# Sample attention on column tiles of 32 instead of 64: one chunk of features to a tile, four chunks side by side

## The chip, the cores and the metric

One Trainium2 chip, one core of it. The time is that of the device, in microseconds (us), for one execution of the whole step; of several runs the median is given.

## What is computed

A two-layer decoder trunk on a prompt of 1024 tokens and on 8 sample sequences of 8 tokens each, whose 2048 earlier keys and values lie in pages of 128 tokens in HBM. The change touches the attention of the samples in layer 0: 8 FoX heads of 64 features (a forget-gate bias is added to the scores) and 4 differential heads, each with two maps of 64 features (`q1.k1`, `q2.k2`) and values of 128 features. Cut to what matters:

```
s  = einsum('bqhd,bkhd->bhqk', qf, kf) * DH_FOX ** -0.5 + cq - ck      # FoX, 8 heads
s2 = einsum('bqhnd,bkhnd->bhnqk', qd, kd) * DH_DIFF ** -0.5            # differential, 4 heads x 2 maps
pf, pd = softmax(s), softmax(s2)          # over 2048 cached keys and the 8 new ones, masked
of = einsum('bhqk,bkhd->bqhd', pf, vf)
od = einsum('bhqk,bkhe->bqhe', pd[:, :, 0] - lam * pd[:, :, 1], vd)
```

For one sequence that is 8 tokens x 8 heads = 64 FoX rows and 8 tokens x 4 heads x 2 maps = 64 differential rows, 128 rows in all, against 2056 keys. All matrix products of the samples' attention are in fp32.

## The kernel before, in words

The work runs in stages: normalisation and projections (to about 285 us), then the last projections (of the values, `proj_v`) merged with the first 24 steps of the samples' attention, then the attention of the prompt merged with the rest of the samples', then output projection, recurrent block and feed-forward layers (from about 900 us).

**Layout.** The 512 FoX features and the 512 differential features of a token are each cut into four chunks `c` of 128; a chunk holds two FoX heads, or one differential head with its two maps. `hp` is the half of a chunk. Keys of a page lie as 128 features by 2 kinds by 4 chunks by 128 tokens (`kc`), values as 128 tokens by 2 kinds by 512 features (`vc`). The 128 rows of scores of a sequence are PSUM partitions: kind 0 (FoX) on partitions 0 to 63, kind 1 (differential) on 64 to 127.

**Scores.** `batch_start` (L825) writes a sequence's queries into `wz` (128 features x 2 kinds x 4 chunks x 64 columns), zero except where a chunk's features meet the rows of its own heads. `key_job` (L836) takes two pages: `load` (L839) reads them into one tile `raw` of 1 MB (two transfers of 512 KB from SyncE's queue; `RAW` = 5 such tiles rotate), and `mm` (L850) issues 8 products: for each chunk and kind, 64 columns of `wz` as the stationary operand, 256 key columns as the moving one, summed over the chunks into 64 partitions. A product with `csel` (L854) first adds the FoX bias from `cm`, which POOL loads (L844). `new_keys` (L867) does the same with the 8 new keys.

**Values.** `value_job` (L895) takes two pages of values: the probabilities are transposed (`turn`, L914), then for each page and kind a product with 64 columns of `pT` as stationary and all 512 features of the kind as moving operand (L932). Of the 64 x 512 that come out, each row needs the features of its own head alone. `end` (L935) scales, `end_sum` (L939) transposes four blocks of 128 and picks the needed parts into `mixs` and `ods`.

**Minus lambda.** `lamc` (L331 to L334) holds 1 for each row, and -lambda on the rows of the second map (partitions 96 to 127 before); `norm` (L889) multiplies it into the reciprocal sums.

**Order of the work.** `sample_jobs` (L951) lists key jobs of one sequence alternating with value jobs of the one before; `pipeline` (L615) runs a job's stages in successive steps (load, start, mm); `merge` (L968) interleaves the sample's steps with the prompt's by their share. SyncE's queue keeps this program order; on the other engines a scheduler sets the order of instructions with its own estimate of their durations. On POOL's queue stand, one behind the other, the loads of `cm`, the loads of the prompt's queries and keys (`load_map`, L590 and L591), and copies.

Of the kernel before, what the change touches and what calls it, by code (L numbers as in the profile page):

```python
# [11 lines left out]
F32 = mybir.dt.float32  # L12
F32R = mybir.dt.float32r
I32 = mybir.dt.int32
AF = mybir.ActivationFunctionType
OP = mybir.AluOpType
AX = mybir.AxisListType
# [5 lines left out]
TS = 64  # L23
T = TP + TS
NB = 8
NQ = 8
# [47 lines left out]
def sub_ap(t, off, dims):  # L74
    return bass.AP(tensor=t.tensor, offset=t.offset + off, ap=[list(t.ap[0])] + [list(d) for d in dims])
# [3 lines left out]
def hybrid_step(ctx: ExitStack, tc: tile.TileContext, xT, w_in, w_fl, w_v, w_out, w_gate, w_x, w_lout, w_ai, ffn_a, ffn_b,  # L79
# [3 lines left out]
    V, S, G, PE, SP = nc.vector, nc.scalar, nc.gpsimd, nc.tensor, nc.sync  # L83
# [38 lines left out]
    ident = const.tile([128, 128], F32, name="ident")  # L122
# [179 lines left out]
    qs = attp.tile([128, 2, 4, TS], F32, name="qs")  # L302
    kn = attp.tile([128, 2, 4, TS], F32, name="kn")
    cqT = attp.tile([128, 8, H], F32, name="cqT")
    lamc = attp.tile([128, 2], F32, name="lamc")
    csel = attp.tile([128, 128], F32R, name="csel")
# [3 lines left out]
    cqc = attp.tile([128, NB], F32, name="cqc")  # L310
# [5 lines left out]
    def attention_consts():  # L316
        SP.dma_start(ptt, ptab)
        SP.dma_start(newm, cst[:, CST["newm"][0]:CST["newm"][1]])
        lamp = tc.alloc_tile_pool(name="lamp", bufs=1, side="right")
        lraw = lamp.tile([128, 4, 64], F32, name="lraw")  # L320
        SP.dma_start(lraw, bass.AP(tensor=lamv.tensor, offset=lamv.offset, ap=[[0, 128], [64, 4], [1, 64]]))
        lsum = lamp.tile([128, 2], F32, name="lsum")
        lpr = lamp.tile([128, 2, 64], F32, name="lpr")
        V.tensor_tensor(lpr, lraw[:, 0:4:2], lraw[:, 1:4:2], op=OP.mult)
        V.tensor_reduce(lsum, lpr, axis=AX.X, op=OP.add)
        lex = lamp.tile([128, 2], F32, name="lex")
        S.activation(lex, lsum, AF.Exp)
        lam_init = 0.8 - 0.6 * math.exp(-0.3 * 0)
        lamt = lamp.tile([128, 1], F32, name="lamt")
        V.tensor_tensor(lamt, lex[:, 0:1], lex[:, 1:2], op=OP.subtract)  # L330
        V.tensor_scalar(lamc[:, 0:1], lamt, lam_init, -1.0, op0=OP.add, op1=OP.mult)  # L331
        lamp.release()
        V.memset(lamc[:, 1:2], 1.0)
        V.tensor_copy(lamc[96:128, 1:2], lamc[96:128, 0:1])  # L334
        V.tensor_scalar(gsub, vcol("subg"), 1.0 - lam_init, None, op0=OP.mult)

    qk_sc = [dram.tile([128, 2, TP], F32R, name=f"qk_sc{i}") for i in range(16)]
# [5 lines left out]
    cq_sc = dram.tile([H, TS], F32, name="cq_sc")  # L343
# [73 lines left out]
    csr = flp.tile([16, 128], F32, name="csr")  # L417
# [93 lines left out]
    for s, n in THIRDS:  # L511
        ps = bank("mm")
# [38 lines left out]
    G.dma_start(cn_sc[1], cl)  # L551
    SP.dma_start(cq_sc, fb[:, TP:])
    for h in range(H):
        SP.dma_start(cqc[h * NQ:h * NQ + NQ, :], bass.AP(tensor=cq_sc.tensor, offset=cq_sc.offset + h * TS, ap=[[1, NQ], [NQ, NB]]))
    S.copy(csel[0:16], csr)
    for i in range(2):
        G.dma_start(cmn[8 * i:8 * i + 8], cn_sc[i])

# [236 lines left out]
    sa1 = tc.alloc_tile_pool(name="sa1", bufs=1, side="right")  # L795
# [3 lines left out]
    mixs = sa1.tile([128, 4, TS], F32, name="mixs")  # L799
    ods = sa1.tile([128, 4, TS], F32, name="ods")  # L800
    bl = sa1.tile([128, KC, TS], F32, name="bl")
    wz = []
    for i in range(2):
        t = sa1.tile([128, 2, 4, 64], F32, name=f"wz{i}")
        G.memset(t, 0.0)
        wz.append(t)
    cms = []
# [17 lines left out]
    def batch_start(bt):  # L825
        b = bt["b"]
        w = bt["w"] = wz[b % 2]
        for kind in range(2):
            for hp in range(2):
                rows = slice(hp * 64, hp * 64 + 64)  # L830
                o, step = (hp * 8, 80) if kind == 0 else (hp * 32, 72)
                S.copy(sub_ap(w[rows], kind * 256 + o, [[step, 4], [1, NQ]]), qs[rows, kind, :, b * NQ:(b + 1) * NQ])
        bt["sx"] = sa.tile([128, PAST + NQ], F32, name="sx")
        bt["mx"] = small.tile([128, 5], F32, name="smx")

    def key_job(bt, g, u):  # L836
        jb = {}

        def load():  # L839
            jb["raw"] = load_keys(bt["b"], 4 * g + 2 * u)  # L840
            if u == 0:
                cm = bt["cm", g] = cms[flip["cm"] % 2]
                flip["cm"] += 1
                G.dma_start(cm[0:16], cs_sc[bt["b"], :, :, 4 * g:4 * g + 4, :].rearrange("i h j k -> (i h) (j k)"))  # L844

        def start():
            if g == 0 and u == 0:
                batch_start(bt)

        def mm():  # L850
            w = bt["w"]
            if u == 0:
                ps = bt["ps", g] = bank("ss")
                PE.matmul(ps, csel, bt["cm", g], start=True, stop=False, skip_group_check=True)  # L854
            ps = bt["ps", g][:, 256 * u:256 * u + 256]
            for c in range(4):
                for kind in range(2):
                    PE.matmul(ps[64 * kind:64 * kind + 64], w[:, kind, c, :], jb["raw"][:, :, kind, c, :], start=False,  # L858
                              stop=(c == 3), skip_group_check=True)

        def evac():
            V.tensor_tensor_reduce(out=bt["sx"][:, 512 * g:512 * g + 512], in0=bt["ps", g], in1=zero.to_broadcast([128, 512]),
                                   scale=1.0, scalar=-3e38, op0=OP.add, op1=OP.max, accum_out=bt["mx"][:, g:g + 1])
        return [load] + [None] * (LEAD - 1) + [start] + [None] * (GAP - 1) + [mm] + [evac] * u

    def softmax_job(bt):
        def new_keys():  # L867
            b, w, sx, mx = bt["b"], bt["w"], bt["sx"], bt["mx"]
            ps = bt["pn"] = bank("ss")
            bq = slice(b * NQ, (b + 1) * NQ)  # L870
            PE.matmul(ps[:, 0:NQ], csel, cmn[:, bq], start=True, stop=False, skip_group_check=True)
            for c in range(4):
                for kind in range(2):
                    PE.matmul(ps[64 * kind:64 * kind + 64, 0:NQ], w[:, kind, c, :], kn[:, kind, c, bq], start=False,
                              stop=(c == 3), skip_group_check=True)

        def top():
            ps, sx, mx = bt["pn"], bt["sx"], bt["mx"]
            V.tensor_tensor_reduce(out=sx[:, PAST:], in0=ps[:, 0:NQ], in1=newm, scale=1.0, scalar=-3e38,
                                   op0=OP.add, op1=OP.max, accum_out=mx[:, 4:5])  # L880
            nm = small.tile([128, 1], F32, name="snm")
            V.tensor_reduce(nm, mx, axis=AX.X, op=OP.max)
            cq = cqc[:, bt["b"]:bt["b"] + 1]
            V.tensor_tensor(nm, nm, cq, op=OP.add)
            V.tensor_tensor(nm, cq, nm, op=OP.subtract)
            bt["ls"] = small.tile([128, 1], F32, name="sls")
            S.activation(sx, sx, AF.Exp, bias=nm, accum_out=bt["ls"])

        def norm():  # L889
            rl = bt["rl"] = sa.tile([128, 1], F32, name="srl")  # L890
            V.reciprocal(rl, bt["ls"])
            V.tensor_tensor(rl, rl, lamc[:, 1:2], op=OP.mult)
        return [None] * (LEAD + GAP) + [new_keys, top, norm]

    def value_job(bt, g, x):  # L895
        jb = {}
# [26 lines left out]
        def mm():  # L923
            if x == 0 and late:
                turn()
            if g == 0 and x == 0:
                bt["po"] = bank("oo")
            pT, po = bt["pT", g], bt["po"]
            for jj in range(n2):
                for kind in range(2):  # L930
                    f = slice(64 * kind, 64 * kind + 64)
                    PE.matmul(po[f], pT[:rows, 2 * x + jj, f], jb["raw"][:rows, jj, kind],  # L932
                              start=(g == 0 and x == 0 and jj == 0), stop=(g == 4), skip_group_check=True)

        def end():  # L935
            bt["ob"] = sa.tile([128, 512], F32, name="ob", bufs=2)
            S.activation(bt["ob"], bt["po"], AF.Copy, scale=bt["rl"])

        def end_sum():  # L939
            b, ob = bt["b"], bt["ob"]  # L940
            bq = slice(b * NQ, (b + 1) * NQ)
            pt = bank("tt", (128, 4, 128))
            for c in range(4):
                PE.transpose(pt[:, c, :], ob[:, c * 128:(c + 1) * 128], ident)
            for hp in range(2):
                rows = slice(hp * 64, hp * 64 + 64)
                V.tensor_copy(mixs[rows, :, bq], sub_ap(pt[rows], hp * 8, [[144, 4], [1, NQ]]))
            V.tensor_reduce(ods[:, :, bq], sub_ap(pt, 64, [[136, 4], [1, NQ], [32, 2]]), axis=AX.X, op=OP.add)
        return [load] + [None] * (LEAD - 1) + [start] + [None] * (GAP - 1) + [mm] + ([end, end_sum] if g == 4 else [])

    def sample_jobs():  # L951
# [838 lines left out]
```

## Time and profile before

| | us |
|---|---|
| median of 3 runs (lowest to highest) | 3138.46 (3134.02 to 3145.78) |
| the profiled execution | 3136.24 |
| its span, first to last instruction | 3134.5 |
| TensorE busy | 2957.0 (94% of the span) |
| VectorE busy | 2100.7 (67%) |
| ScalarE busy | 1324.4 (42%) |
| GpSimd busy | 398.9 (13%) |

A row of a group of instructions reads: line, engine, operation, tile written <- tiles read, shape of operand, number of instructions. PE is TensorE's matmul, PEld its load of the stationary operand, SPq, POOLq and PEldq the instruction queue of the engine. An fp32 product of the program stands in the trace as two MATMUL records, each behind a load of its own, one for each pass of the fp32 product; one of kind fp32r (written `f32` in the rows too) is one record, and so is a transpose. "128\*64" is a stationary operand of 128 rows by 64 columns. A matmul's end is modelled, and consecutive ones overlap, so the time from start to start is what one costs.

### The profile page before, as it was taken

To read this page: it belongs to the slowest core of one execution; us is meant where nothing else is said; L and a number is where in the kernel's file an instruction comes from. 1 tells how busy PE (TensorE), PEld (TensorE's weight loads), DVE (VectorE), ACT (ScalarE), POOL (GpSimd) and SP (SyncE) were. 2 spreads that over 40 slices of the span, in tenths; PEclk is the share of its full clock that TensorE was granted. 3 is DMA by queue.
4 is the path that set the end of the run, shared out by engine and by line. 5 is a ranking of instruction groups with operands and counts; after the bars stand their busy time and mean duration, and the time that the engine had idled before them with its cause. 6 is when DMAs were issued, how large, how long until landed. Compare 5 with 4: busy or idle time off the path is not lost. (4 is left out here: it accounts for less than half of the span.)

```text
span 3134.5 us, 58133 instructions
## 1 busy us (share of the span) xinstructions
PE 2957.0 (94%) x21141; PEld 2709.5 (86%) x21141; DVE 2100.7 (67%) x4435; ACT 1324.4 (42%) x2477; POOL 398.9 (13%) x817
## 2 busy tenths in 40 slices
PE   7989999999997899899999999999969999999997
PEld 6988856565577899899999999999969899999997
DVE  6563134443458679988856777768785998886567
ACT  4111234444445533343344555555454334344444
POOL 0100010000000112321200011211011222221000
PEclk8999999999998999999999999999979999999999
DMA  4878688898785456544586652325735664448566
GB/s 147 238 226 308 208 324 306 308 338 319 274 263 191 161 174 207 199 143 140 175 269 193 216 184 96 100 97 167 262 126 172 221 209 161 151 145 260 181 187 212
DMA packets 383473, 646.96 MB, mean 206 GB/s; under 512 B 40305, under 2 KB 210690, under 8 KB 381138
## 3 DMA queue, kind: packets, MB, share of 16 engines
q1 hardware_dynamic: 321234, 478.65, 47.6%
q0 software_dynamic: 41792, 141.52, 12.2%
q10 hardware_dynamic: 20160, 23.07, 2.2%
q8 instruction: 166, 2.72, 0.4%
q14 instruction: 121, 0.99, 0.1%
HBM read 476.15 MB, written 166.95 MB: 205 GB/s over the span
## 5 line engine op out<-in xcount | busy, mean ns | idle before, releaser
L1060 ACT CAST b_hi<-b_raw 128x512 fp32r<-128x512 f32 (+1 forms) x645 | 394.8, 616 | 599.7 <-PE mm L1367 236.7
L136 DVE TENSOR_TENSOR b_lo<-b_raw,b_hi 128x512 fp32r<-128x512 f32 (+1 forms) x645 | 439.0, 683 | 236.6 <-ACT b_hi L1060 231.8
L1367 PE MATMUL mm<-d_lo,b_hi 128*128 128x272 f32 x1848 | 526.3, 293 | 4.6 <-DVE d_lo L136 4.5
L1368 PE MATMUL mm<-d_hi,b_lo 128*128 128x272 f32 x1848 | 525.2, 293 | 0.0
L1366 PE MATMUL mm<-d_hi,b_hi 128*128 128x272 f32 x1848 | 479.5, 297 | 40.7 <-ACT d_hi L1360 31.7
L1366 PEld LDWEIGHTS mm<-d_hi,b_hi 128*128 128x128 f32 x1848 | 331.4, 195 | 46.5 <-ACT d_hi L1360 40.6
L1367 PEld LDWEIGHTS mm<-d_lo,b_hi 128*128 128x128 f32 x1848 | 356.5, 193 | 6.4 <-DVE d_lo L136 6.2
L1368 PEld LDWEIGHTS mm<-d_hi,b_lo 128*128 128x128 f32 x1848 | 355.1, 193 | 0.0
L136 DVE TENSOR_TENSOR d_lo<-d_raw,d_hi 128x544 fp32r<-128x544 f32 (+1 forms) x297 | 175.5, 594 | 56.4 <-ACT d_hi L1360 55.2
L1360 ACT CAST d_hi<-d_raw 128x544 fp32r<-128x544 f32 (+1 forms) x297 | 160.8, 543 | 106.4 <-DMA d_raw<-a_b 50.0
L1082 PE MATMUL mm<-hh,b_hi 128*128 128x364 f32 (+1 forms) x480 | 158.5, 331 | 3.7 <-ACT b_hi L1060 3.1
L1083 PE MATMUL mm<-hl,b_hi 128*128 128x364 f32 (+1 forms) x480 | 157.6, 330 | 0.0
L1084 PE MATMUL mm<-hh,b_lo 128*128 128x364 f32 (+1 forms) x480 | 151.3, 330 | 0.0
L160 PE MATMUL mm<-hh,w_hi 128*128 128x364 f32 (+1 forms) x384 | 127.9, 335 | 14.4 <-DVE ev L296 7.9
L932 PE MATMUL oo<-raw,pT 128*64 128x512 f32 (+1 forms) x544 | 138.6, 604 | 1.1 <-ACT pT L921 1.1
L1211 PE MATMUL mm<-b22h,b_hi 128*128 128x272 f32 x384 | 115.0, 299 | 24.4 <-DVE bt L1294 24.4
L858 PE MATMUL ss<-raw,wz 128*64 128x256 f32 x1024 | 137.4, 389 | 0.0
L1271 ACT ACTIVATE ft<-ft 128x544 f32<-128x544 f32 x96 | 63.9, 666 | 169.1 <-DVE ft L1270 168.9
L161 PE MATMUL mm<-hl,w_hi 128*128 128x364 f32 (+1 forms) x384 | 127.9, 335 | 1.6 <-DVE hl L254 1.6
L162 PE MATMUL mm<-hh,w_lo 128*128 128x364 f32 (+1 forms) x384 | 127.3, 333 | 0.0
L675 ACT ACTIVATE st<-st,nb 128x128 f32<-128x128 f32 (+7 forms) x128 | 98.1, 768 | 55.2 <-DVE nb L669 29.4
L1212 PE MATMUL mm<-b22l,b_hi 128*128 128x272 f32 x384 | 114.1, 297 | 0.0
(401 smaller groups left out, 8401.6 us busy)
## 6 DMA issues: line engine op xcount, KB each, us to landing
raw<-in_kc SPq DMA_DIRECT2D x128, 512.0 KB
raw<-in_vc SPq DMA_DIRECT2D x128, 512.0 KB
b_raw<-w_sum SPq DMA_DIRECT2D x174, 256.0 KB
b_raw<-in_ffn_d SPq DMA_DIRECT2D x168, 256.0 KB
b_raw<-in_ffn_a SPq DMA_DIRECT2D x144, 256.0 KB
a_t<-ts POOLq DMA_DIRECT2D x116, 272.0 KB, 4.0
b_raw<-in_ffn_b SPq DMA_DIRECT2D x96, 256.0 KB
d_raw<-a_t SPq DMA_DIRECT2D x87, 272.0 KB
```

The lines of the kernel that those rows point to most:

```text
L136: (eng or V).tensor_tensor(out, x, hi, op=OP.subtract)
L160: PE.matmul(ps[:, :n], hi[:, k, :], rh[:, s:s + n], start=(k == order[0]), stop=False)
L858: PE.matmul(ps[64 * kind:64 * kind + 64], w[:, kind, c, :], jb["raw"][:, :, kind, c, :], start=False, stop=(c == 3), skip_group_check=True)
L932: PE.matmul(po[f], pT[:rows, 2 * x + jj, f], jb["raw"][:rows, jj, kind], start=(g == 0 and x == 0 and jj == 0), stop=(g == 4), skip_group_ ...
L1060: S.copy(hi, raw)
L1082: PE.matmul(ps[:, :n], hi, rh[:, s:s + n], start=(k == order[0]), stop=False)
L1083: PE.matmul(ps[:, :n], hi, rl[:, s:s + n], start=False, stop=False)
L1084: PE.matmul(ps[:, :n], lo, rh[:, s:s + n], start=False, stop=(k == order[-1]))
L1360: S.copy(rh, raw)
L1366: PE.matmul(p, wh[:, m, :], rh[:, s], start=(start and j == 0), stop=False, skip_group_check=True)
L1367: PE.matmul(p, wh[:, m, :], rl[:, s], start=False, stop=False, skip_group_check=True)
L1368: PE.matmul(p, wl[:, m, :], rh[:, s], start=False, stop=(j == nj - 1), skip_group_check=True)
```

## The change

The score rows are ordered by chunk: partition 32c + 8hp + q holds FoX head 2c + hp, and 32c + 16 + 8hp + q map `hp` of differential head c. Each chunk's products then write one band of 32 partitions, with `tile_position=(0, 32 * c)`.

- Scores: still 8 products of 256 columns for a key job, now with 32 stationary columns, kind outside and chunk inside, so that four products in a row go to four different column tiles. `wz` is half as wide.
- Values: for each page four products of 256 columns (the chunk's 128 FoX and 128 differential features) with 32 stationary columns, in place of two of 512 with 64.
- At a sequence's end 256 columns are scaled and two blocks transposed, not 512 and four.
- -lambda goes to partitions 32c + 24 to 32c + 31 by four small DMAs on POOL's queue, in place of one copy on VectorE; `cqc` and `csel` follow the new order of rows.

In the changed file lines 335 to 829 of before stand two lower, and those from 833 on one lower (L858 is L859 there, L932 is L933).

```
@@ attention_consts
-        V.tensor_copy(lamc[96:128, 1:2], lamc[96:128, 0:1])
+        for c in range(4):
+            r = slice(32 * c + 24, 32 * c + 32)
+            G.dma_start(lamc[r, 1:2], lamc[r, 0:1])
...
-        SP.dma_start(cqc[h * NQ:h * NQ + NQ, :], bass.AP(...))
-    S.copy(csel[0:16], csr)
+        SP.dma_start(cqc[32 * (h // 2) + 8 * (h % 2):32 * (h // 2) + 8 * (h % 2) + NQ, :], bass.AP(...))
+    S.copy(csel[0:16].rearrange("k (c a r) -> k c a r", c=4, a=2)[:, :, 0], csr[:, :64].rearrange("k (c r) -> k c r", c=4))
...
-        t = sa1.tile([128, 2, 4, 64], F32, name=f"wz{i}")
+        t = sa1.tile([128, 2, 4, 32], F32, name=f"wz{i}")
@@ batch_start
-                o, step = (hp * 8, 80) if kind == 0 else (hp * 32, 72)
-                S.copy(sub_ap(w[rows], kind * 256 + o, [[step, 4], [1, NQ]]), qs[rows, kind, :, b * NQ:(b + 1) * NQ])
+                S.copy(sub_ap(w[rows], kind * 144 + hp * 8, [[32, 4], [1, NQ]]), qs[rows, kind, :, b * NQ:(b + 1) * NQ])
@@ key_job, mm (new_keys likewise, with 0:NQ columns of kn)
-            for c in range(4):
-                for kind in range(2):
-                    PE.matmul(ps[64 * kind:64 * kind + 64], w[:, kind, c, :], jb["raw"][:, :, kind, c, :], start=False,
-                              stop=(c == 3), skip_group_check=True)
+            for kind in range(2):
+                for c in range(4):
+                    PE.matmul(ps[32 * c:32 * c + 32], w[:, kind, c, :], jb["raw"][:, :, kind, c, :], start=False,
+                              stop=(kind == 1), tile_position=(0, 32 * c), skip_group_check=True)
@@ value_job, mm
-                for kind in range(2):
-                    f = slice(64 * kind, 64 * kind + 64)
-                    PE.matmul(po[f], pT[:rows, 2 * x + jj, f], jb["raw"][:rows, jj, kind],
-                              start=(g == 0 and x == 0 and jj == 0), stop=(g == 4), skip_group_check=True)
+                for c in range(4):
+                    f = slice(32 * c, 32 * c + 32)
+                    PE.matmul(po[f, 0:256], pT[:rows, 2 * x + jj, f], jb["raw"][:rows, jj, :, 128 * c:128 * c + 128],
+                              start=(g == 0 and x == 0 and jj == 0), stop=(g == 4), tile_position=(0, 32 * c), skip_group_check=True)
@@ value_job, end and end_sum
-            S.activation(bt["ob"], bt["po"], AF.Copy, scale=bt["rl"])
+            S.activation(bt["ob"][:, :256], bt["po"][:, :256], AF.Copy, scale=bt["rl"])
...
-            for c in range(4):
-                PE.transpose(pt[:, c, :], ob[:, c * 128:(c + 1) * 128], ident)
+            for kind in range(2):
+                PE.transpose(pt[:, kind, :], ob[:, kind * 128:(kind + 1) * 128], ident)
```

How TensorE's order moves is shown at the place where the projections of values end and the prompt's first scores follow. Before (`raw,wz` are scores of cached keys, `raw,pT` values, `ident,sx` transposed probabilities, `qk` the prompt's scores):

```order
L854 MATMUL ss<-cm_2319,csel 128x512
L858 MATMUL ss<-raw,wz_2315 64x256 x16
L919 MATMUL tt<-ident,sx 128x128 x4
L919 MATMUL tt<-ident,sx 8x128
L932 MATMUL oo<-raw,pT 64x512 x9
L652 MATMUL ss<-qk 128x128
L654 MATMUL ss<-mask,identr 128x128
```

and with the change:

```order
L859 MATMUL ss<-raw,wz_2318 32x256 x16
L920 MATMUL tt<-ident,sx 128x128 x4
L920 MATMUL tt<-ident,sx 8x128
L933 MATMUL oo<-raw,pT 32x256 x16
L654 MATMUL ss<-qk 128x128
L656 MATMUL ss<-mask,identr 128x128
```

The products of a job stay together, as 32 columns by 256 in both kinds of job; the bias product L854 of this group moved to an earlier place.

On POOL's queue, at the same place, the prompt's first loads (`qk`, `kl`) stood behind nine loads of `cm`, before:

```order
L844 DMA cm_2319<-cs_sc 16x512
L844 DMA cm_2317<-cs_sc 16x512
L590 DMA qk<-qk_sc_92 128x2048
L591 DMA kl<-kl_sc_108 128x1024
L590 DMA qk<-qk_sc_93 128x2048
L591 DMA kl<-kl_sc_109 128x1024
```

and stand behind ten with the change:

```order
L845 DMA cm_2320<-cs_sc 16x512
L845 DMA cm_2322<-cs_sc 16x512
L592 DMA qk<-qk_sc_92 128x2048
L593 DMA kl<-kl_sc_108 128x1024
L592 DMA qk<-qk_sc_93 128x2048
L593 DMA kl<-kl_sc_109 128x1024
```

One more load of `cm`, which waits for the bias product two groups back, is now ahead of the prompt's first loads.

## Rows read from the trace of the kernel before

**Rows 1.** The page: span and busy time of TensorE and its weight loads, VectorE, ScalarE and GpSimd over the whole run; and of the DMA issues the one that loads pages of keys.

```profile
span 3134.5 us, 58133 instructions
PE 2957.0 (94%) x21141; PEld 2709.5 (86%) x21141; DVE 2100.7 (67%) x4435; ACT 1324.4 (42%) x2477; POOL 398.9 (13%) x817
...
raw<-in_kc SPq DMA_DIRECT2D x128, 512.0 KB
```

**Rows 2.** Stretches of the two merged stages: from and to, length, busy us of PE, PEld, DVE, ACT and POOL with the number of instructions, then the granted share of TensorE's clock, the DMA engines' busy share and GB/s.

```profile
285.00:350.00 65.00, 65.00 (x519) 51.07 (x519) 6.92 (x19) 13.21 (x24) 0.97 (x2) 1.00 0.81 305
350.00:400.00 50.00, 50.00 (x375) 40.40 (x376) 3.85 (x6) 8.38 (x15) 0.49 (x1) 1.00 0.55 177
400.00:450.00 50.00, 48.89 (x293) 26.74 (x291) 17.96 (x81) 17.52 (x44) 6.08 (x15) 0.93 0.94 343
450.00:500.00 50.00, 50.00 (x333) 29.55 (x332) 18.90 (x82) 24.25 (x56) 3.57 (x8) 1.00 0.80 277
500.00:550.00 50.00, 50.00 (x297) 30.73 (x295) 21.18 (x82) 20.23 (x46) 4.82 (x11) 1.00 0.92 347
550.00:600.00 50.00, 49.83 (x323) 29.19 (x322) 22.50 (x99) 24.97 (x58) 5.07 (x11) 1.00 0.94 347
600.00:650.00 50.00, 50.00 (x318) 30.16 (x316) 22.49 (x85) 23.19 (x51) 3.43 (x7) 1.00 0.90 323
650.00:700.00 50.00, 50.00 (x316) 31.59 (x315) 23.20 (x92) 19.35 (x44) 4.33 (x11) 1.00 0.84 300
700.00:750.00 50.00, 47.99 (x297) 27.59 (x294) 18.34 (x81) 22.92 (x55) 2.35 (x5) 0.97 0.79 276
750.00:800.00 50.00, 49.77 (x335) 33.07 (x335) 23.70 (x108) 22.43 (x49) 5.57 (x13) 1.00 0.93 344
800.00:850.00 50.00, 50.00 (x309) 27.49 (x305) 17.09 (x63) 19.65 (x46) 3.03 (x7) 1.00 0.86 318
850.00:900.00 50.00, 48.45 (x265) 27.38 (x265) 20.53 (x78) 24.66 (x50) 0.00 (x0) 1.00 0.64 212
```

**Rows 3.** The two stages again, for the instructions of one line alone (busy us of PE and PEld with the number of records; clock, DMA share and GB/s are the stretch's): first the products of cached keys, L858, then those of values, L932.

```profile
285.00:400.00 115.00, 28.54 (x224) 15.18 (x224) 1.00 0.69 249
400.00:900.00 500.00, 108.87 (x800) 57.38 (x800) 0.99 0.85 309
...
285.00:400.00 115.00, 11.40 (x48) 3.00 (x48) 1.00 0.69 249
400.00:900.00 500.00, 127.22 (x496) 33.08 (x496) 0.99 0.85 309
```

**Rows 4.** TensorE's matmuls in order of time, some 15 us of the second stage: start, length from the first start to the last end, what, how many records.

```profile
498.88 0.60 PE L944 MATMUL tt<-ident,ob 128*128 128x128 f32 x4
...
500.43 0.40 PE L652 MATMUL ss<-qk 128*128 128x512 f32 x1
500.67 0.39 PE L655 MATMUL ss<-kl,qk 128*128 128x512 f32 x1
...
502.12 3.65 PE L932 MATMUL oo<-raw,pT 128*64 128x512 f32 x16
505.71 1.13 PE L714 MATMUL tt<-pf,v 128*128 128x256 f32 x4
...
507.14 0.40 PE L854 MATMUL ss<-cm,csel 128*128 128x512 f32 x1
507.47 0.65 PE L858 MATMUL ss<-raw,wz 128*64 128x256 f32 x2
508.05 0.92 PE L714 MATMUL tt<-pf,v 128*128 128x256 f32 x4
508.90 3.67 PE L858 MATMUL ss<-raw,wz 128*64 128x256 f32 x30
```

**Rows 5.** The same view, one line: the products of one sequence's 8 new keys (8 moving columns).

```profile
314.77 0.64 PE L874 MATMUL ss<-kn,wz 128*64 128x8 f32 x16
```

**Rows 6.** From the list of waits on SyncE's queue from 285 to 900 us (who waited <- for what: us in total, times, longest): L818 issues the loads of pages. Then, from the view of the instructions that read or write `raw`, 400 to 900 us, what ended the idle time before them where it was a page's landing (us, times).

```profile
SPq L818 <- PE ss L858: 114.9, 35, 9.2
SPq L818 <- PE oo L932: 108.3, 41, 12.1
...
  DMA raw<-in_vc: 0.7, 3
```

**Rows 7.** Four successive stretches of 20 us, columns as in rows 2.

```profile
500.00:520.00 20.00, 20.00 (x113) 11.48 (x112) 10.04 (x37) 9.76 (x19) 2.66 (x5) 1.00 1.04 408
520.00:540.00 20.00, 20.00 (x117) 12.52 (x117) 6.78 (x26) 6.77 (x19) 1.32 (x4) 1.00 0.98 378
540.00:560.00 20.00, 20.00 (x142) 12.62 (x141) 9.86 (x56) 9.53 (x21) 1.63 (x5) 1.00 0.61 187
560.00:580.00 20.00, 19.83 (x130) 12.21 (x129) 11.39 (x38) 11.25 (x24) 3.31 (x7) 1.00 1.03 390
```

**Rows 8.** The instructions on `lamc`, with shortest, median and longest ns, and first and last start in us: the copy that the change removes, and the multiplication that reads the column (L892, in `norm`). Then POOL's first load of the prompt's queries and keys in order of time; in brackets, how long POOL's queue had been idle, and until what.

```profile
L334 DVE COPY lamc<-lamc x1: 149/149/149, 27.0 to 27.0; 32x1 f32<-32x1 f32 x1
L892 DVE TENSOR_TENSOR srl<-srl,lamc x8: 151/159/161, 320.3 to 858.5; 128x1 f32<-128x1 f32 x8
...
400.79 0.58 POOL L590 DMA_DIRECT2D qk<-qk_sc  x1 [34.98 <-PE ss L854]
```

More of the change, by code (lines that the diff above doesn't have):

```diff
@@ L553, in hybrid_step @@
     for h in range(H):
-        SP.dma_start(cqc[h * NQ:h * NQ + NQ, :], bass.AP(tensor=cq_sc.tensor, offset=cq_sc.offset + h * TS, ap=[[1, NQ], [NQ, NB]]))
-    S.copy(csel[0:16], csr)
+        SP.dma_start(cqc[32 * (h // 2) + 8 * (h % 2):32 * (h // 2) + 8 * (h % 2) + NQ, :], bass.AP(tensor=cq_sc.tensor, offset=cq_sc.offset + h * TS, ap=[[1, NQ], [NQ, NB]]))
+    S.copy(csel[0:16].rearrange("k (c a r) -> k c a r", c=4, a=2)[:, :, 0], csr[:, :64].rearrange("k (c r) -> k c r", c=4))
     for i in range(2):
@@ L871, in new_keys @@
             PE.matmul(ps[:, 0:NQ], csel, cmn[:, bq], start=True, stop=False, skip_group_check=True)
-            for c in range(4):
-                for kind in range(2):
-                    PE.matmul(ps[64 * kind:64 * kind + 64, 0:NQ], w[:, kind, c, :], kn[:, kind, c, bq], start=False,
-                              stop=(c == 3), skip_group_check=True)
+            for kind in range(2):
+                for c in range(4):
+                    PE.matmul(ps[32 * c:32 * c + 32, 0:NQ], w[:, kind, c, :], kn[:, kind, c, bq], start=False,
+                              stop=(kind == 1), tile_position=(0, 32 * c), skip_group_check=True)
         def top():
@@ L929, in mm @@
             for jj in range(n2):
-                for kind in range(2):
-                    f = slice(64 * kind, 64 * kind + 64)
-                    PE.matmul(po[f], pT[:rows, 2 * x + jj, f], jb["raw"][:rows, jj, kind],
-                              start=(g == 0 and x == 0 and jj == 0), stop=(g == 4), skip_group_check=True)
+                for c in range(4):
+                    f = slice(32 * c, 32 * c + 32)
+                    PE.matmul(po[f, 0:256], pT[:rows, 2 * x + jj, f], jb["raw"][:rows, jj, :, 128 * c:128 * c + 128],
+                              start=(g == 0 and x == 0 and jj == 0), stop=(g == 4), tile_position=(0, 32 * c), skip_group_check=True)
         def end():
             bt["ob"] = sa.tile([128, 512], F32, name="ob", bufs=2)
-            S.activation(bt["ob"], bt["po"], AF.Copy, scale=bt["rl"])
+            S.activation(bt["ob"][:, :256], bt["po"][:, :256], AF.Copy, scale=bt["rl"])
         def end_sum():
@@ L942, in end_sum @@
             pt = bank("tt", (128, 4, 128))
-            for c in range(4):
-                PE.transpose(pt[:, c, :], ob[:, c * 128:(c + 1) * 128], ident)
+            for kind in range(2):
+                PE.transpose(pt[:, kind, :], ob[:, kind * 128:(kind + 1) * 128], ident)
             for hp in range(2):
                 rows = slice(hp * 64, hp * 64 + 64)
-                V.tensor_copy(mixs[rows, :, bq], sub_ap(pt[rows], hp * 8, [[144, 4], [1, NQ]]))
-            V.tensor_reduce(ods[:, :, bq], sub_ap(pt, 64, [[136, 4], [1, NQ], [32, 2]]), axis=AX.X, op=OP.add)
+                V.tensor_copy(mixs[rows, :, bq], sub_ap(pt[rows], hp * 8, [[32, 4], [1, NQ]]))
+            V.tensor_reduce(ods[:, :, bq], sub_ap(pt, 144, [[32, 4], [1, NQ], [8, 2]]), axis=AX.X, op=OP.add)
         return [load] + [None] * (LEAD - 1) + [start] + [None] * (GAP - 1) + [mm] + ([end, end_sum] if g == 4 else [])
```

## The prediction

> **What bounds the kernel now.** I read the page first: TensorE is busy for 2957.0 of 3134.5 us, every other engine much less [rows 1]. That is an average, so next the table by stretches of the two stages in which the samples' attention runs, 285 to 900 us [rows 2]. Here PE is busy from edge to edge in nearly every stretch, while VectorE and ScalarE are at most half busy. The column to watch is another one: the DMA engines, at 0.79 to 0.94 from 400 to 850 us. The waits say how the two stand to each other: SyncE's loads of pages waited 114.9 us for the score products and 108.3 us for the value products, that is for a free `raw` tile, while PE's idle time that a page's landing ended is under a microsecond [rows 6]. So TensorE sets the pace now, and the transfers follow at 85% of what they can do after 400 us [rows 3]. A faster TensorE asks them for more.
>
> **What the narrow products cost now.** The two lines that change hold 1024 score records and 544 value records, by the counts of [rows 3]. In order of time [rows 4] 16 value records take 3.65 us, the last alone 0.6, so 3.05 / 7 = 0.43 us for two, start to start; 30 score records take 3.67 us, the last 0.38 of it, 3.29 / 14 = 0.235 for two. A value product moves 512 columns and a score product 256; half of 0.43 is 0.22, and I take that for the scores. For a full-width fp32 product of 256 columns the same view has four records in 1.13 us, the last 0.38 of it: some 0.22 us for one. So with 64 columns two records run at once, one on each half of the array. Are they two passes of one product, or the products of two kinds? One row decides: a score product that stands alone is two records in 0.65 us, which is 0.27 plus the 0.38 that one lasts, so its passes ran one after the other (at 507.47 us) [rows 4]. What runs side by side are two column tiles, and for that the second tile's first pass must start while the first tile's second pass, ahead of it in the program, is still waiting.
>
> **Removed from TensorE.** Scores: 512 pairs x 0.22 us = 113 us. Values: 272 pairs x 0.43 us = 117 us. Together 230 of the 276 us that the two lines are busy [rows 3]; the rest is filling and draining at each block's ends, and stays. With the change the score jobs have as many records of as many columns, the value jobs twice as many of half the columns. If four tiles run at once, four records share 0.22 us: 256 + 272 such groups, 528 x 0.22 = 116 us. That saves 114 us: by the counts of rows 3, 112 pairs x 0.11 + 24 x 0.215 = 17 us before 400 us, and 400 x 0.11 + 248 x 0.215 = 97 us after. Is the issue of so many short instructions a limit? The products of new keys, with 8 columns, show 16 matmuls and their 16 weight loads in 0.64 us, the last 0.2 of it [rows 5]: about 14 ns an instruction. A group of four is 8 instructions, 0.11 us, below the 0.22 us that its columns take. The new keys themselves have as many instructions as before: no gain.
>
> **Smaller edits.** A sequence's end saves two transposes of 0.11 us (at 498.88 us) [rows 4], eight times: 2 us, taken as it is; the shorter copy, the narrower `wz` and the other partitions of `cqc` and `csel` cost nothing, on engines half idle [rows 2]. The four DMAs for -lambda are issued at 27 us on POOL and needed first at 320 us [rows 8]; the column could be 290 us late before anyone waited. What they replace on VectorE is 149 ns.
>
> **Added to TensorE.** Widths change more often. By the order of instructions the stream goes from one width (128, 64, 32) to another 368 times before and 422 times after, because the prompt's products of 64 columns now stand beside blocks of 32. The lone block shows the price of a change: its first load stands 0.33 us behind the start of the 512-column product before it, where the next such product follows after 0.24 (at 507.14 and 500.43 us) [rows 4]; and the load after it comes 0.58 us after its start, where its two passes need 0.44. So 0.1 us for a change, 54 x 0.1 = 5 us; 3 where TensorE is still the bound.
>
> **What the transfers leave of it.** The pages' bytes are the same, so a stretch can get no shorter than its DMA busy time. The idle DMA time of the ten stretches after 400 us, length x (1 - share) [rows 2], is 3, 10, 4, 3, 5, 8, 10.5, 3.5, 7 and 18 us. TensorE would save 97 us there, 9.7 a stretch. The smaller of the two, stretch by stretch, is 3 + 9.7 + 4 + 3 + 5 + 8 + 9.7 + 3.5 + 7 + 9.7 = 62.6 us. That lets transfers shift freely within 50 us. They can't quite: five tiles of 1 MB are held, and at 400 GB/s [rows 7] a tile takes 2.6 us, so the stock is 13 us. At 20 us the shares are 1.04, 0.98, 0.61 and 1.03 [rows 7]; the smaller of 3.9 and the idle time is 0, 0.4, 3.9 and 0, 4.3 us in 80, which over 500 us would be 27. I take 50, nearer to 62.6, as a faster TensorE frees tiles earlier in the loose stretches and asks for the next there. Before 400 us the shares of 0.81 and 0.55 [rows 2] leave 35 us, more than the 17 that TensorE saves, which count in full.
>
> Where TensorE waits for pages its clock can fall. In the stretch from 400 us, the one with the lowest granted clock, 0.93 [rows 2], a seventh of 50 us was at the lower level, 1.2 in place of 2.4 GHz; that costs 3.5 us. One or two more such falls: 5 us.
>
> **The sum.** 17 + 50 + 2 - 3 - 5 = 61 us. The profiled execution took 3136.2 us, its span 3134.5 and 1.7 around it; 2.2 us under the median of 3138.5. 3136.2 - 61 = 3075; at the median's level 3077. I say **3076 us**. The ends of this case: with 27 in place of 50, and 12 in place of 17, it saves 33 us (3103); if the transfers were evened out over the whole of the second stage, up to its idle 72 us, some 95 us (3041).
>
> One rule of the Trainium skill would size the terms otherwise: TensorE: Matmul & The Clock Gate, Part 3, Measured speedup, gives 2.38x for three column tiles. An estimate from it: four tiles would win 4 x 0.79 = 3.2 over one, TensorE would save 86 us and the kernel some 50. The rows show for two tiles nearly the full factor.
>
> **The rivals.**
> *Two at a time still.* If the array, or what feeds it, takes only two streams, a job costs what it costs now, plus the 5 us of width changes: 3136.2 + 5 = 3141, no change. For it: no row has more than two at work. Against it: the dispatch past a waiting pass exists for two tiles [rows 4], and four need the same thing thrice. Its decision point: the length of a full block of 16 score records, 2.0 us if two run at once, 1.1 if four.
> The skill's rule in TensorE: Matmul & The Clock Gate, Part 3, What overlaps and what doesn't, is that matmuls are strictly first in, first out; then each tile's second pass would hold back the next tile, one product would need one 0.22 us step, and this rival would come true. The trace disagrees: 16 value records took eight steps (3.65 us), not the nine of such an order (4.1).
> *The transfers give nothing.* If the rate stays where it is after 400 us, because loads are issued in the program's order and each waits for its tile, the wait moves from SyncE to TensorE and only the first stage's 17 us remain, less 3 and 5: some 9 to 17 us, 3119 to 3127. For it: four stretches of rows 2 stand at 0.92 to 0.94. Against it: 408 GB/s is reached [rows 7] where 309 is the mean [rows 3].
> *One at a time: slower.* If narrow products with a named tile position don't overlap at all, each record costs its own 0.22 us: 1024 + 1088 records, 465 us in place of 230, with the width changes 240 us more on an engine that bounds the stage: 3136 + 240 = 3376. It decides from fewer than two tiles at work on average. For it: the overlap seen so far is of a form without such a position. Against it: those tiles too are bands of output partitions, only wider.
> *The prompt starts late.* Its first loads are now behind one more `cm` load on POOL. They went out at 400.79 us, when the projections ended [rows 8]; the bias products for which the added load waits stand ahead of the last projections in TensorE's order, so I put nothing.
>
> **How the numbers follow.** Forecast case 0.72; two at a time 0.14; transfers give nothing 0.08; one at a time 0.06. Half a per cent (16 us) is about what a measurement of this kernel can tell from no change. Faster: nearly all of the first (0.71) and half of the third (0.04), 0.75. The same: 0.14 + 0.04, 0.18. Slower: the fourth, and a little of the first, 0.07. The range runs from the forecast's lower end to the point of no change, 3041 to 3140: it leaves out the fourth case and the upper half of the second.
>
> **What would show it.** Right: 16 records of 32 columns in about 1.1 us, the two lines' busy time from 276 to some 160 us, the end of the second stage 60 us earlier, DMA shares of 0.95 in most of its stretches, SyncE's waits for the two lines well below 223 us, and PE's idle time by page landings in tens of us. Wrong: blocks of 16 score records still at 2.0 us; or the blocks short, but the stage as long as before, with TensorE waiting for something other than pages, VectorE or ScalarE above all.

## The result, and the profile after

The changed kernel takes 3061.9 us (median of 4 runs, 3060.3 to 3067.4) against 3140.7 for the kernel before beside it: ratio 0.9753, 95% interval 0.973 to 0.9777, faster by 79 us. Forecast were 3076 us and a range of 3041 to 3140. The profiled execution took 3062.7 us, 73.6 less than the one of before.

First the page: span and busy times, to set beside [rows 1].

```profile
span 3060.9 us, 59156 instructions
PE 2855.8 (93%) x21669; PEld 2659.7 (87%) x21669; DVE 2102.1 (69%) x4434; ACT 1326.3 (43%) x2477; POOL 402.8 (13%) x821
```

TensorE is busy 101 us less, with 528 matmul records more (544 more of values, 16 fewer transposes). Next its matmuls in order of time, where [rows 4] and [rows 5] stand for before (L859 are scores of cached keys, L875 those of new keys, L933 values).

```profile
446.24 1.07 PE L859 MATMUL ss<-raw,wz 128*32 128x256 f32 x16
449.32 1.07 PE L859 MATMUL ss<-raw,wz 128*32 128x256 f32 x16
...
453.36 0.31 PE L875 MATMUL ss<-kn,wz 128*32 128x8 f32 x16
...
454.19 0.64 PE L933 MATMUL oo<-raw,pT 128*32 128x256 f32 x8
```

A block of 16 score records, the two passes of eight products, takes 1.07 us: 0.38 for the last and 0.69 for three steps, 0.23 each. Two at a time would take 2.0 us. Eight value records take 0.64, one step and the last. Four column tiles run at once.

The table of the two lines, as in [rows 3]; the projections of values end at 380 us now (400 before) and the last value product at 816 (893).

```profile
285.00:380.00 95.00, 14.53 (x208) 5.54 (x208) 1.00 0.79 289
380.00:816.00 436.00, 54.34 (x800) 21.83 (x800) 0.96 0.96 356
...
285.00:380.00 95.00, 7.04 (x96) 2.62 (x96) 1.00 0.79 289
380.00:816.00 436.00, 77.91 (x992) 23.45 (x992) 0.96 0.96 356
```

Their busy time fell from 276 us to 154 (one block of scores, 1 us, now lies before 285 us). The clock and the DMA share are the other half of the story. Here is the whole second stage, from the end of the projections to the last value product, columns as in [rows 2]: before in the first row, after in the second, then four stretches after.

```profile
400.00:893.50 493.50, 489.98 (x3037) 289.81 (x3036) 205.52 (x842) 215.57 (x493) 38.25 (x87) 0.99 0.87 313
...
380.00:816.00 436.00, 409.42 (x3558) 251.11 (x3557) 206.28 (x851) 218.55 (x499) 37.67 (x86) 0.96 0.96 356
...
500.00:550.00 50.00, 48.82 (x448) 28.76 (x445) 22.26 (x89) 27.54 (x61) 4.92 (x12) 1.00 1.01 374
550.00:600.00 50.00, 44.38 (x386) 27.71 (x379) 29.10 (x116) 25.00 (x62) 5.01 (x11) 0.93 1.01 369
600.00:650.00 50.00, 50.00 (x458) 31.67 (x457) 21.21 (x86) 23.95 (x52) 4.64 (x11) 1.00 1.02 391
650.00:700.00 50.00, 44.76 (x352) 28.41 (x351) 26.79 (x101) 25.02 (x57) 4.13 (x8) 0.93 0.91 337
```

Over the stage the DMA engines' share went from 0.87 to 0.96, and the granted clock from 0.99 to 0.96. Three of the four stretches have no DMA time left, and two of the four show TensorE idle for over 5 us with the clock down. The clock's records have five falls to its lower level in this stage, 34 us in all; before, they have two, 10 us in all. Narrow windows show them, first the five, then the two of before:

```profile
390.00:400.00 10.00, 7.40 (x55) 4.54 (x54) 4.23 (x26) 5.22 (x16) 0.80 (x2) 0.50 1.05 395
492.00:496.00 4.00, 3.93 (x26) 2.65 (x26) 2.60 (x17) 0.48 (x1) 0.00 (x0) 0.57 1.03 372
588.00:595.00 7.00, 5.61 (x23) 4.99 (x22) 3.42 (x18) 3.41 (x13) 1.08 (x3) 0.51 1.04 394
690.00:697.00 7.00, 6.10 (x31) 3.78 (x32) 2.00 (x4) 1.17 (x2) 0.00 (x0) 0.53 1.05 392
786.00:793.00 7.00, 5.73 (x36) 3.59 (x37) 3.06 (x6) 4.69 (x10) 0.00 (x0) 0.51 1.00 397
...
414.00:421.00 7.00, 7.00 (x21) 4.03 (x22) 4.18 (x22) 5.26 (x12) 1.05 (x3) 0.51 1.04 394
714.00:718.00 4.00, 3.43 (x15) 2.81 (x17) 0.50 (x2) 2.75 (x6) 0.32 (x1) 0.57 0.81 270
```

The waits say what TensorE and the loads wait for (who waited <- for what: us, times, longest). First SyncE's queue in the second stage before (400 to 893.5 us), then after (380 to 816 us); in the fence behind it, TensorE's own idle time before matmuls in the second stage after.

```profile
SPq L818 <- PE ss L858: 94.3, 30, 7.6
SPq L818 <- PE oo L932: 93.8, 37, 12.1
SPq L818 <- DMA raw<-in_kc: 0.4, 1, 0.4
...
SPq L820 <- PE ss L859: 48.4, 26, 4.3
SPq L820 <- PE oo L933: 43.1, 30, 7.7
SPq L820 <- DMA raw<-in_vc: 19.5, 15, 3.3
SPq L820 <- DMA raw<-in_kc: 17.4, 6, 6.7
```

```profile
PE ss L654 <- DMA qk<-qk_sc: 5.7, 3, 2.6
PE tt L732 <- DVE st L700: 5.2, 5, 3.3
PE ss L657 <- DMA kl<-kl_sc: 3.4, 2, 2.0
PE ss L654 <- DVE mx L658: 3.2, 6, 1.0
```

The loads of pages wait 92 us for TensorE instead of 188, and now also for earlier pages to land (37 us against 0.4). TensorE does not wait much for pages: its idle time that they ended stays near 5 us over both stages. It waits for the prompt's queries and keys, 9 us, and for VectorE and ScalarE, the prompt's chain above all, some 15 us.

### The profile page after: what moved, and what is told of

The parts are those of the page before. It is cut to its first block, busy times and chain, and to the rows that moved or that the text cites. A ratio compares the mean times of both kernels' runs of the same rounds, so it can differ in the third digit from the quotient of the medians.

```text
span 3060.9 us, 59156 instructions
## 1 busy us (share of the span) xinstructions
PE 2855.8 (93%) x21669; PEld 2659.7 (87%) x21669; DVE 2102.1 (69%) x4434; ACT 1326.3 (43%) x2477; POOL 402.8 (13%) x821
## 5 line engine op out<-in xcount | busy, mean ns | idle before, releaser
L1367 PE MATMUL mm<-d_hi,b_hi 128*128 128x272 f32 x1848 | 486.1, 297 | 46.4 <-ACT d_hi L1361 34.2
L1214 PE MATMUL mm<-b22h,b_lo 128*128 128x272 f32 x384 | 115.8, 302 | 0.0
L1212 PE MATMUL mm<-b11h,b_hi 128*128 128x272 f32 x384 | 111.8, 291 | 0.0
```

The lines of the kernel that those rows point to most:

```text
L1212: PE.matmul(p[:, :NT], hi[:, k, :], rh, start=(start and k == 0), stop=False, skip_group_check=True)
L1367: PE.matmul(p, wh[:, m, :], rh[:, s], start=(start and j == 0), stop=False, skip_group_check=True)
```

## The experiments

All ratios are to the kernel before, run beside each kernel; the changed kernel's is 0.9753, and 0.9757 in a second measurement.

### Each half of the change alone

`keys_only` keeps the old value products, `values_only` the old score products (those of the new keys too, and the wider `wz`).

```
keys_only, value_job mm:      for kind: PE.matmul(po[64*kind ...], pT[..., f], raw[:rows, jj, kind], ...)      # 64 x 512, as before
values_only, key_job mm:      for c: for kind: PE.matmul(ps[64*kind ...], w[:, kind, c, :], ...)               # 64 x 256, as before
```

> The change for the scores alone: score products on four column tiles of 32, value products as before (two per page, 64 columns of probabilities by 512 features); the values' outputs then mix rows, only the time counts. Theory (TensorE saved some 120 us, the transfers kept a third of it): half the saving meets less of the transfers' limit, so it gets more than half of the full change's 77 us: about 45 us, 3093 us. Rival (each part gets its share of what chains between the engines allow): half, 39 us, 3100 us or above. Both: 16 score records in about 1.1 us, L859 busy about 69 us, value products still about 139 us.

> The change for the values alone: value products on four column tiles of 32, score products in the old form (64 columns, chunk outside, kind inside); the rows of scores then stand in the old order, only the time counts. Theory: about 43 us saved, 3096 us, so that the two halves alone add up to more (88 us) than the whole change (77). Rival: 38 us or less, and the sum at or below 77.

Measured: 3101.2 us, ratio 0.9895 (0.9877 to 0.9912), and 3097.1 us, 0.9875 (0.9857 to 0.9892). That is 33 and 39 us, together 72, within the error of the whole change's 77. The theory had expected more than half from each half, and this was a miss: the two parts add up. The second stage took 472 and 456 us (493 before, 436 with both). The traced execution of `values_only` took 3106.3 us, 9 over its median. The changed lines, as in [rows 3], first the scores of `keys_only`, then the values of `values_only`:

```profile
380.00:852.00 472.00, 57.15 (x800) 21.93 (x800) 0.97 0.90 327
...
393.00:849.00 456.00, 74.89 (x988) 24.26 (x992) 0.98 0.92 338
```

So already half the change lost much of its gain there: the scores alone cut their own line from 109 to 57 us in that stage and the stage by 21, with the DMA engines idle for a tenth of it. The prediction's smaller of two numbers per stretch (TensorE's saving, idle DMA time) is too simple: the loss sets in well before the stage's idle DMA time is used up.

### Are the transfers the limit? Fewer of them, and more

`half_after` and `half_before` leave out every second load of value pages, in the changed kernel and in the one before; `quarter_after` the same of keys as well; `extra_after` and `extra_before` load 33.5 MB twice.

```
half_*:     def load():  if x == 1: jb["raw"] = bt["vraw"]; return          # the tile of the job before
quarter_after, also:  if u == 0: bt["kraw"] = load_keys(...)
                      jb["raw"] = bt["kraw"]
extra_*:    if g < 4 and x == 0: load_pages(bt["b"], 4 * g, vc, more..., ...)  # a tile of its own, not read
```

> The changed kernel with every second load of value pages left out (the second value job of a group uses the tile of the first; 32 of 256 MB... that is 64 loads of 512 KB, 33.5 MB, are not made, and these values are wrong). Theory (transfers limit the second stage now): 30 to 45 us less than the changed kernel, 3062 to about 3025 us, DMA share in the second stage at 0.8 to 0.9, SyncE's waits for the products up again. Rival (TensorE's own order and its partners limit it): within 8 us of the changed kernel.

> The kernel before with the same loads left out. Theory: TensorE set the pace there, so the transfers cost little: 0 to 10 us less than before, 3130 to 3141 us. Rival (transfers were a limit before as well): over 20 us less.

> The changed kernel with every second load of pages left out for keys and values (67 MB in all; these scores and values are wrong). With half of that left out the second stage took 413 us and TensorE was busy for 400 of it. If that is TensorE's own floor, the stage stays at 400 to 413 us and the whole within 0 to 12 us of that kernel, 3030 to 3042 us. If transfers still held it, another 15 us or more go.

> The changed kernel with 33.5 MB more of transfers: each value job with x = 0 also loads its two pages into a tile of its own that nothing reads (64 loads of 512 KB, some 84 us of DMA at 400 GB/s). If the transfers are what the second stage now lacks (DMA busy 0.96 of its 436 us): 45 to 75 us slower than the changed kernel, 3105 to 3135 us. If TensorE's order and its partners hold it: under 20 us slower.

> The kernel before with the same loads added. Its two stages had some 100 us of idle DMA time, 65 of it in the second: 5 to 35 us slower than before, clearly less than the changed kernel loses. If the two lose the same, the transfers bind both alike.

| | us | ratio (95%) | second stage, us |
|---|---|---|---|
| half_before | 3136.7 | 1.0009 (0.9997 to 1.0021) | 499 |
| half_after | 3041.6 | 0.9691 (0.9666 to 0.9717) | 413 |
| quarter_after | 3043.6 | 0.9707 (0.9676 to 0.9738) | 421 |
| extra_before | 3172.2 | 1.0127 (1.0091 to 1.0162) | 532 |
| extra_after | 3123.5 | 0.9968 (0.9953 to 0.9984) | 506 |

The second stage of each, columns as in [rows 2]: `half_before`, `half_after`, `quarter_after`, `extra_before`, `extra_after`, one fence each.

```profile
397.00:896.00 499.00, 496.23 (x3034) 294.56 (x3034) 205.92 (x842) 215.99 (x493) 37.96 (x87) 0.99 0.72 250
```

```profile
377.00:790.00 413.00, 400.08 (x3508) 252.09 (x3506) 201.93 (x842) 211.95 (x492) 37.60 (x86) 0.98 0.85 302
```

```profile
379.00:800.00 421.00, 408.01 (x3519) 256.97 (x3517) 204.35 (x842) 213.07 (x493) 37.97 (x87) 0.96 0.67 232
```

```profile
394.00:926.00 532.00, 507.88 (x3101) 294.33 (x3099) 214.87 (x867) 224.23 (x505) 38.33 (x87) 0.97 0.95 352
```

```profile
379.00:885.00 506.00, 438.19 (x3588) 266.04 (x3586) 213.00 (x867) 223.41 (x505) 37.82 (x86) 0.91 0.98 368
```

Before, leaving out transfers gives nothing (TensorE busy 496 of 499 us, in an execution 16 us over the median): TensorE set the pace, as forecast. After, it gives 19 us (0.0062 of 3140), less than the 30 to 45 expected and more than the rival's 8. Leaving out twice as much gives no more: `quarter_after` lies a little above both of its ranges, with the DMA engines at 0.67 and TensorE busy for 408 of 421 us. So with fewer transfers the stage takes 413 to 421 us, 15 to 23 less than in the real kernel.

That size need not be the transfers' alone. Leaving out loads also made the scheduler place TensorE's instructions anew: set line by line beside the changed kernel's, the sequence of TensorE's records in these two traces differs in 2900 and 3100 lines. Three kernels with all loads and an order changed as much, at the end of this section, have stages 9 to 15 us longer than the changed kernel's.

Adding transfers costs the changed kernel 67 us of the 84 that the loads take, with the DMA engines at 0.98, well beyond the 16 to 27 us by which those three kernels are slower. The stage grew by 70 us: TensorE's idle time by 41, its busy time by 29. About as much was lost to the clock, 28 us (0.09 of 506 us instead of 0.04 of 436). The kernel before loses 40, a little over its range, though it had some 65 us of idle DMA time in the stage. So the transfers do bind now, and they bound little before.

### How far TensorE looks past a waiting product

`same_tile` puts four records in a row on the same column tile.

```
-            for kind in range(2):
-                for c in range(4):
+            for c in range(4):
+                for kind in range(2):
                     PE.matmul(ps[32 * c:32 * c + 32], w[:, kind, c, :], ..., tile_position=(0, 32 * c), ...)
```

> The changed kernel with the score products in the order chunk outside, kind inside, so that four records in a row go to one column tile; the values stay as changed. How far does TensorE look past a waiting record? If far (per-tile order with a deep queue): a block of 16 records still takes about 1.1 us and the time stays within 5 us. If one waiting record per tile can be passed: some 10 steps of 0.22 us, 2.4 us a block, 64 x 1.3 = 85 us more TensorE work, 40 to 80 us slower than the changed kernel. If none: 13 steps, 3.0 us, 70 to 120 us slower.

Measured: 3064.8 us, ratio 0.9775 (0.9759 to 0.9792), 4 to 7 us over the changed kernel. A block, in order of time:

```profile
284.65 1.09 PE L859 MATMUL ss<-raw,wz 128*32 128x256 f32 x16
```

1.09 us where the changed order took 1.07. The records that start in its first 0.15 us:

```profile
284.65 0.44 PE L859 MATMUL ss<-raw,wz 128*32 128x256 f32 x4
```

Four records start within 0.04 us, one on each tile, and the next only at 284.89. So TensorE starts the fourth tile's first pass though three records of each tile ahead of it wait. That the scheduler kept the written order inside the block is read from the starts alone: successive tiles start 13 ns apart here and 7 ns in the changed kernel, as fits twice as many records between them. For these score products, what makes the tiles run together is that they are different tiles, not the order in which kind and chunk are written. The 4 to 7 us are no clean price of that order, because TensorE's sequence also changed elsewhere (810 lines).

### More buffers, and an earlier start of the prompt

> The changed kernel itself, unedited, beside the three that follow: 0.975 of before, as measured.

> The changed kernel with eight page tiles in place of five (RAW = 8). If the transfers' unevenness within some 20 us is what holds the second stage (DMA busy 0.96 of it, five tiles are 13 us of transfers), a stock of 21 us evens it out: 5 to 15 us less than the changed kernel, not more than 17, because DMA busy time is 419 of the stage's 436 us. If other engines and the prompt's chain hold it: within 3 us.

> The changed kernel with three buffers for the prompt's queries and keys in place of two (QKB = 3). TensorE waited 9 us for them (5.7 and 3.4). If these waits are a cause of their own, 5 to 9 us less; if they are only where the full DMA engines show, the same bytes still have to come and it stays within 3 us.

> A version meant to be faster, with nothing left out: the changed kernel with the prompt's query and key tiles in a pool opened before the projections of values end, so that the first loads (6 us of transfers, now issued when the projections end, at 381 us) go out in the first stage, where the DMA engines are at 0.79. The stretch after 380 us, where TensorE has idle time and its clock fell for 10 us, should go: 5 to 12 us less than the changed kernel, ratio to before 0.972 to 0.974. If the new order of instructions or the full DMA engines take it back: within 4 us of the changed kernel, 0.975.

```
raw8:      RAW = 8          qkb3:   QKB = 3
pq_early:  pqk = tc.alloc_tile_pool(name="pqk", bufs=1, side="right")   # ahead of the merge with the projections; qk and kl in it
```

The changed kernel again: 3060.7 us, 0.9757 (0.9739 to 0.9774). The others are all slower than it: `raw8` 3083.4 us, 0.9822 (0.9794 to 0.985); `qkb3` 3076.4, 0.981 (0.9794 to 0.9827); `pq_early` 3083.1, 0.9842 (0.9815 to 0.9868). All three expectations failed. Their second stages take 451, 448 and 445 us, at DMA shares of 0.93 to 0.95. Where TensorE waited, in `raw8` and in `pq_early`:

```profile
PE tt L716 <- ACT pf L735: 8.7, 10, 2.7
PE ss L872 <- DVE mx L658: 6.2, 2, 5.9
PE oo L933 <- ACT pT L922: 4.5, 6, 1.7
```

```profile
PE tt L732 <- ACT pf L735: 7.6, 2, 4.8
PE tt L945 <- ACT ob L938: 4.6, 2, 4.0
PE tt L732 <- DVE st L700: 4.4, 2, 3.8
```

These are waits for ScalarE and VectorE, not for data. In `pq_early` the prompt's first loads did go out early, at 273 us instead of 381, and TensorE's matmuls no longer wait for them in the stage; the time grew all the same. The scheduler places the instructions by its own estimates, and each of these edits made it place them anew: between `raw8` and the changed kernel over 2000 lines of TensorE's order differ. So the runs don't isolate a buffer, and whether a deeper stock of pages would help in an unchanged order stays open. That the new order is what made them slower is the likeliest reading and not shown by itself. The stages are 9 to 15 us longer, the whole kernels 16 to 27 us: in `raw8` and `pq_early` 14 and 7 us more were lost behind the last value product. That much scatter is to be allowed for in the comparisons above; two traces of the changed kernel itself differ by 3 us in the stage. No version tried beats the changed kernel with its work left whole.

## Why the prediction was right, and where its sizes were off

- **Four at once: right.** 1.07 us for a block where 1.1 was expected, 154 us for the two lines where 160 was. The rivals "two at a time" and "one at a time" are ruled out by the block's length, and `same_tile` shows the dispatch that the first of them doubted.
- **TensorE's saving: in line with the 114 us at the two lines (122), but not all of it is time.** In the second stage the two lines fell by 104 us, where 97 was expected. The rest of TensorE's busy time rose from 254 to 277 us, and its idle time from 3.5 to 26.6: 104 - 23 - 23 = 58, the 493.5 - 436 us by which the stage shrank. With half of the value loads gone (`half_after`, the two lines below) the lines fell by 99, and 9 + 9 us of such losses remained: 80 us; in `quarter_after` the stage shrank by 73. So with fewer transfers the new products are worth 73 to 80 us to the stage, not 97, with the scatter of another order on that.

```profile
377.00:790.00 413.00, 64.43 (x800) 24.44 (x800) 0.98 0.85 302
...
377.00:790.00 413.00, 72.81 (x984) 29.15 (x984) 0.98 0.85 302
```

- **What the transfers take: the mis-sized term.** The sum let them take 47 of 97 us and leave 50. By `half_after` and `quarter_after` it is 15 to 23, as far as these runs can part it from a new order; that the transfers bind at all rests on `extra_after`. That the stage would end near its DMA time was right: 0.96 of 436 us is 419, close to the 428 of before. The other part of the loss, in the clock, in TensorE's own order and in its partners, had 8 us in the sum (5 for the clock, 3 for changes of width).
- **The total: in part luck.** The sum had 44 us for the second stage (50 + 2 - 3 - 5), and the stage shrank by 58. It came that near because a term too large for the transfers made up for terms too small for the clock and the rest.
- **The first stage: right in size.** The projections end 20 us earlier, 2 to 3 of them because they started that much earlier; 17 were expected.
- **The clock: too small.** 5 us were set. 0.04 of 436 us was lost to it, against 0.01 of 493.5 before: some 12 us more, part of it while TensorE waited anyway. So up to 12 of the 23 us by which the rest of TensorE's busy time rose are the clock. The other 11 stay open: 53 more changes of width in the stage, at the forecast's 0.1 us each, would be 5.
- **Behind the stage:** the last value product comes 78 us earlier and the end 74, with the same work in between; 4 us went in layers that the change doesn't touch.
- **What would show it.** SyncE's waits for the two lines fell from 223 us to 121 over both stages, and from 188 to 92 in the second: right. The second stage ended 78 us earlier where 60 was said. That TensorE would wait tens of us for pages was wrong: it waits 9 us for the prompt's loads and some 15 us for VectorE and ScalarE. The rival that the transfers give nothing fell: 356 GB/s in the stage where 313 were.
- **Small edits: as said, with one exception.** The four DMAs on `lamc` end long before the first reading at 315 us. The new keys' products, put at no gain, halved: 0.31 us for 16 records instead of 0.64.
- **Slips in the working that change no conclusion.** The range's lower end takes some 95 us as saved, where 17 + 72 + 2 is 91 with nothing taken off: 3045, not 3041. The full-width row gives (1.13 - 0.38) / 3 = 0.25 us a record, not 0.22; the first of its three steps took longer than the rest. TensorE's idle time that landing pages ended was 0.7 us for values and 0.5 for keys, a little over a microsecond.

## What to carry to other kernels

Products whose useful output is a block diagonal should be laid out so that each block has a column tile of its own: the same columns then cost a quarter of the array's time instead of half, and the order in which the score products' tiles were written hardly mattered. Before counting the gain, read in the same stretches how much DMA time is idle, and test it by leaving out and adding loads, in the kernel before as well: the same loads cost 40 us there and 67 here. Where a scheduler sets the order, an edit meant to free one wait moves thousands of instructions, and its measured effect is that of the edit and the whole new order; the same holds for an experiment that leaves out loads.

## What the runs showed of the hardware

The 14 ns an instruction that [rows 5] gave is not a rate of issue: the same 16 matmuls and 16 loads, now with 32 stationary columns on four tiles, took 0.31 us instead of 0.64. Eight steps of two records, 0.06 us each, became four steps of four, 0.04 us each. Fewer steps and narrower loads came together here, so no run shows how much of it is the loading of the stationary operand.

Records on four tiles ran in steps of 0.23 us for 256 columns, the 0.22 to 0.235 that two tiles took. With fp32 operands on all 128 rows the two further streams cost nothing that these rows show.

TensorE's idle time and the time at the lower clock level grew together, though not in step. In the second stage of before, `half_after`, `quarter_after`, the changed kernel and `extra_after` TensorE was idle for 3.5, 13, 13, 27 and 68 us, and the clock's records have 10, 17, 31, 34 and 96 us at the lower level. So the stages in which TensorE waited more also lost more to the clock; no run here parts cause and effect.
